# Value products of the DMA-transposed probability chunks: three 16-bit matmuls, or two 32-bit matmuls behind a GpSimd conversion

## The chip, the cores and the metric

The kernel runs on one core of one Trainium2 chip. The metric is the device time of one execution in microseconds (us); lower is better. Five engines work on the core at the same time, each through its own instructions in a fixed order: PE (TensorE, matrix products; PEld is its weight load), DVE (VectorE), ACT (ScalarE), POOL (GpSimd), and SP, which here only issues DMA transfers. An engine that waits for one instruction holds back everything behind it in its own order.

## The reference

One layer of an encoder is computed for two sequences, a sample of 512 tokens and a prompt of 1024 tokens, with model width 1024. What the change touches is the softmax attention of branch A: 8 query heads of width 64, in two groups of four that share one key and one value head each.

```python
def _gqa_attention(q, k, v):
    ...
    def block(qi):
        s = jnp.einsum('bqkgd,bskd->bkgqs', qi, k, preferred_element_type=jnp.float32) * scale
        p = jax.nn.softmax(s, axis=-1)
        return jnp.einsum('bkgqs,bskd->bqkgd', p.astype(v.dtype), v)
```

Everything is float32. The rest (projections, rotary embedding, a neighbourhood attention as branch B, gates, an MLP of width 4096, a final norm) is the same in both kernels.

## The kernel before

The kernel holds 32-bit accuracy with matmuls on split numbers: a value is cut into a high part in the 32-bit matmul format (`F32R`) and the remainder as a low part, and products of the parts are summed in PSUM. It runs the sample trunk, then the prompt trunk (`run`), then the MLP of both. Only the prompt trunk (`NB == 2`, so `ND = 4`) is touched.

In the prompt trunk each of the two head groups g has a phase phR, which projects q, k and v, rotates q and k, and writes the values into `vhl` (per chunk of 128 keys: 64 columns high part, 64 columns low part), and then a phase phA, the attention. phA walks over eight units of (head h, half of the queries qb); a unit is 512 queries against 1024 keys, that is eight key chunks. While the products of a unit are made, the scores of the next unit are computed (`s_tile`, four per unit, one per 128 queries):

- PE makes the scores (tile `ss`, four matmuls); DVE takes the negated row maximum (`nms`); ACT the exponential with its row sum (`ps`, `ls`); DVE the reciprocal (`rls`); POOL multiplies it by 2^14 (`rcs`).
- The last four key chunks go the DMA way: ACT writes `hls` high = p times `rcs` in float16, DVE the float16 remainder, and an SP-issued transposing DMA puts both into `PTs` (high and low plane of each chunk, keys on the partitions).
- The first four key chunks go the PE way: POOL normalises them (`pns`), and `turn` transposes them on PE (four 128x128 transposes into `pTs`), ACT copies the high part (`pths`) and DVE the remainder (`ptls`).

`pv` adds the value products of one chunk to the unit's accumulator `os`. For a PE-way chunk these are two matmuls with `vhl` (on `pths`, on `ptls`); for a DMA-way chunk three with 16-bit operands, straight from `PTs`: weights `vpls`, a bfloat16 three-part split of the value chunk that phR writes for the last four token tiles in `rotate` (ACT, DVE, two POOL operations per tile, and one memset per group). After the eighth chunk, `finish_o` adds the two halves and stores them.

Between these, `fill.pull` puts single k-steps (three matmuls into `gpss`) of the gate projection into PE's order, so that PE has work that depends on nothing in the unit: six k-steps per unit. The table `PLAN` gives, for each of eight slots of a unit, how many turns, how many scores of the next unit and how many products are emitted in program order. From program order a scheduler makes the final order of each engine; what is shown of orders below is that final one. Buffers: `pths` and `ptls` two each, `PTs` two, `hls` two, `pns` seven.

Of the kernel before, what the change touches and what calls it, by code (L numbers as in the profile page):

```python
# [10 lines left out]

F32 = mybir.dt.float32
F32R = mybir.dt.float32r
BF16 = mybir.dt.bfloat16
F16 = mybir.dt.float16
# [14 lines left out]
    (1, 1, (0, 0)),  # L30
    (1, 1, (0, 0)),
    (0, 0, (1, 0)),
    (1, 1, (1, 0)),
    (1, 0, (0, 1)),
    (0, 1, (1, 0)),
    (0, 0, (1, 1)),
    (0, 0, (0, 2)),
# [36 lines left out]
def encoder(ctx: ExitStack, tc: tile.TileContext, xs, outs, w):  # L74
# [367 lines left out]
    def run(tr, nxt, first):  # L442
# [79 lines left out]
        aside = ExitStack()  # L522
        if ND:
            vps = aside.enter_context(phase(f"vp{N}"))
        for g in range(2):
            with phase(f"phR{N}_{g}") as ph:
# [108 lines left out]
                if ND:  # L635
                    vpl = vps.tile([P, ND, 4, HD], BF16, tag="vp", name=f"vpl{N}_{g}", bufs=1)
# [46 lines left out]
                for tt in range(NT):  # L683
# [55 lines left out]
                    def rotate(tt, nm, z, zq, r, rt, pin):  # L739
                        if ND:  # L740
                            t6 = ph.tile([P, 6, HD], F32, tag="t", name=f"t{nm}", bufs=3)
                            t = t6[:, 0:5, :]
                        else:
                            t = ph.tile([P, 5, HD], F32, tag="t", name=f"t{nm}", bufs=2)
# [6 lines left out]
                        if tt >= NP:  # L751
                            if tt == NP:
                                tc.keep_in_program_order(nc.gpsimd.memset(vpl[:, :, 3, :], 0.0))
                            nc.scalar.activation(vpl[:, tt - NP, 0, :], z[:, 320:384], AF.Copy, scale=1.0 / PSC)
                            vr = t6[:, 5, :]
                            nc.vector.scalar_tensor_tensor(
                                vr, z[:, 320:384], 1.0 / PSC, vpl[:, tt - NP, 0, :], op0=ALU.mult, op1=ALU.subtract
                            )
                            nc.gpsimd.tensor_copy(vpl[:, tt - NP, 1, :], vr)
                            nc.gpsimd.tensor_tensor(vpl[:, tt - NP, 2, :], vr, vpl[:, tt - NP, 1, :], op=ALU.subtract)  # L760
                        else:
                            nc.scalar.activation(vhl[:, tt, 0:HD], z[:, 320:384], AF.Copy)
                            nc.vector.tensor_tensor(
                                vhl[:, tt, HD:P], z[:, 320:384], vhl[:, tt, 0:HD].bitcast(F32), op=ALU.subtract
                            )
# [12 lines left out]
                        if ND:  # L778
                            nc.vector.tensor_tensor(t, t, u, op=ALU.add)
                            nc.gpsimd.tensor_copy(t6[:, 5, :], t[:, 4, :])  # L780
                            rr_of[tt] = t6
                        else:
                            rr = ph.tile([P, 6, HD], F32, tag="rr", name=f"rr{nm}", bufs=3)
                            nc.vector.tensor_tensor(rr[:, 0:5, :], t, u, op=ALU.add)
                            nc.gpsimd.tensor_tensor(rr[:, 5, :], t[:, 4, :], u[:, 4, :], op=ALU.add)
                            rr_of[tt] = rr
# [27 lines left out]
            with phase(f"phA{N}_{g}") as ph:  # L814
# [3 lines left out]
                def s_tile(u, j):  # L818
# [33 lines left out]
                    pn = ph.tile([P, NP * P], F32, tag="PN", name=f"pn{nm}", bufs=7)  # L852
# [5 lines left out]
                def turn(u, kc):  # L858
# [5 lines left out]
                    nb = 2 if ND else 3  # L864
# [4 lines left out]
                    return hi, lo  # L869

# [21 lines left out]
                for j in range(4):  # L892
                    s_tile(units[0], j)
                    fill.pull(3 if ND else 2)
                queue = []
                for ui, u in enumerate(units):
                    h, qb = u
                    if first:
# [1137 lines left out]
```

## Time and profile before

| | |
|---|---|
| median of 3 runs (range) | 2125.79 us (2123.9 to 2126.83) |
| profiled execution: time, span | 2125.93 us, 2124.1 us |
| PE busy | 2100.1 us (99%) |
| DVE, ACT, POOL busy | 1473.8, 1122.3, 376.6 us (69%, 53%, 18%) |
| first score of the prompt's attention to its last value product, group 0, group 1 | about 450 to 569 us, 641 to 758 us |
| PE instructions / POOL instructions | 10775 / 590 |

The profiled execution is one run with the hardware profiler; its span runs from the first to the last instruction. "Busy" of PE is not PE at its peak, since matmuls overlap and the recorded end of a matmul lies behind the start of the next. In the rows of groups the columns are: line, engine, operation, output and inputs, shape, count, then busy time and mean ns of one, then the idle time ahead of them and what ended it. Buffer numbers are left out in the names.

### The profile page before, as it was taken

How to read it: one execution, taken by the hardware profiler on the slowest of the kernel's cores; microseconds unless marked ns; L12 is line 12 of the kernel's file. 1: busy time of each engine (PE TensorE's matmuls, PEld its weight loads, DVE VectorE, ACT ScalarE, POOL GpSimd, SP SyncE). 2: the span in 40 equal slices, each digit the busy share in tenths (PEclk: the TensorE clock that was granted, in tenths of full speed). 3: DMA queues.
4: the chain of work that ended last, by engine and by line, in shares of the span. 5: the costliest groups of instructions: out<-in, count | busy, mean ns of one | idle time of the engine just before them, and what ended most of it. 6: DMA issues, size and time to landing. Idle time of an engine off the chain costs nothing.

```text
span 2124.1 us, 31653 instructions
## 1 busy us (share of the span) xinstructions
PE 2100.1 (99%) x10775; PEld 1816.9 (86%) x10775; DVE 1473.8 (69%) x2810; ACT 1122.3 (53%) x2351; POOL 376.6 (18%) x590
## 2 busy tenths in 40 slices
PE   9999999999999999999999999999999999999998
PEld 8887778987796778888888999999999988888887
DVE  6675687777667755557772877778777777759563
ACT  5664664567547744555531666566555633334352
POOL 3232420432232223443201100002000000000000
PEclk9999999999999999999999999999999999999999
DMA  6435567644535443434473656578444799688561
GB/s 187 138 114 156 151 186 247 199 112 93 119 102 118 107 126 94 118 102 124 145 240 109 198 196 205 159 236 214 156 155 153 261 354 342 216 271 277 176 197 71
DMA packets 387178, 367.68 MB, mean 173 GB/s; under 512 B 98752, under 2 KB 322632, under 8 KB 387017
## 3 DMA queue, kind: packets, MB, share of 16 engines
q1 hardware_dynamic: 345079, 295.65, 46.4%
q10 hardware_dynamic: 36258, 52.98, 7.2%
q0 software_dynamic: 5680, 17.04, 2.9%
q8 instruction: 85, 1.39, 0.3%
q14 instruction: 76, 0.62, 0.1%
HBM read 264.85 MB, written 87.88 MB: 166 GB/s over the span
## 4 chain that ended last, share of the span: by engine, by line
PE 52%; DVE 1%; DMA 1%; ACT 1%; issue 0%; POOL 0%; ACTq 0%; POOLq 0%; DVEq 0%
PE dn L216 7%; PE dn L217 7%; PE dn L215 7%; PE uc L215 2%; PE ud L215 2%; PE ud L217 2%; PE uc L217 2%; PE ud L216 2%; PE uc L216 2%; PE ua L217 2%; PE ua L215 2%; PE ua L216 2%; PE ops L217 1%; PE ops L216 1%; PE ops L215 1%; PE ub L215 1%
## 5 line engine op out<-in xcount | busy, mean ns | idle before, releaser
L217 PE MATMUL dn<-wd,al 128*128 128x512 f32 (+1 forms) x624 | 242.3, 388 | 0.0
L216 PE MATMUL dn<-wd,ah 128*128 128x512 f32 (+1 forms) x624 | 242.3, 388 | 0.0
L215 PE MATMUL dn<-wd,ah 128*128 128x512 f32 (+1 forms) x624 | 242.3, 388 | 0.0
L1449 ACT ACTIVATE ah<-ar 128x512 fp32r<-128x512 f32 x168 | 104.5, 628 | 199.7 <-PE dn L216 184.8
L1450 DVE TENSOR_TENSOR al<-ar,ah 128x512 fp32r<-128x512 f32 x168 | 115.5, 694 | 72.8 <-ACT ah L1449 65.1
L215 PEld LDWEIGHTS dn<-wd,ah 128*128 128x128 f32 x624 | 117.2, 188 | 24.4
L216 PEld LDWEIGHTS dn<-wd,ah 128*128 128x128 f32 x624 | 117.2, 188 | 24.1
L217 PEld LDWEIGHTS dn<-wd,al 128*128 128x128 f32 x624 | 117.2, 188 | 24.0
L200 POOL TENSOR_TENSOR rs_f<-ms_f,mhalf 128x1 f32<-128x1 f32 x6 | 4.0, 666 | 590.7 <-DVE ms_f L196 590.7
L829 DVE TENSOR_REDUCE nms<-ss 128x1 f32<-128x1024 f32 (+1 forms) x96 | 99.7, 1040 | 12.0 <-PE ss L827 11.5
L832 ACT ACTIVATE ps<-ss,nms 128x1024 f32<-128x1024 f32 (+1 forms) x96 | 93.0, 969 | 26.5 <-DVE nms L829 12.9
L215 PE MATMUL gpss<-xs_0h,w_gs 128*128 128x512 f32 x256 | 103.5, 404 | 1.5 <-DVE ptls L868 1.3
L217 PE MATMUL gpss<-xs_0h,w_gs 128*128 128x512 f32 x256 | 100.8, 394 | 0.0
L216 PE MATMUL gpss<-xs_0l,w_gs 128*128 128x512 f32 x256 | 100.8, 394 | 0.0
L1449 ACT ACTIVATE A<-S 128x512 fp32r<-128x512 f32 x128 | 76.1, 624 | 32.1 <-DVE S L1512 26.6
L1450 DVE TENSOR_TENSOR A<-S,A 128x512 fp32r<-128x512 f32 x128 | 84.5, 686 | 4.8 <-ACT A L1449 4.8
L1568 ACT ACTIVATE c<-c 128x384 f32<-128x384 f32 x97 | 50.7, 524 | 68.8 <-DVE c L1567 68.5
L215 PE MATMUL uc<-B,A 128*128 128x384 f32 x256 | 85.6, 334 | 1.2 <-ACT s L1584 1.2
L215 PE MATMUL ud<-B,A 128*128 128x384 f32 x256 | 85.6, 334 | 0.0
L217 PE MATMUL ud<-B,A 128*128 128x384 f32 x256 | 85.5, 334 | 0.0
L216 PE MATMUL ud<-B,A 128*128 128x384 f32 x256 | 85.5, 334 | 0.0
L216 PE MATMUL uc<-B,A 128*128 128x384 f32 x256 | 85.5, 334 | 0.0
(376 smaller groups left out, 6396.5 us busy)
## 6 DMA issues: line engine op xcount, KB each, us to landing
ar<-ud SPq DMA_DIRECT2D x120, 512.0 KB
br<-in_w_mlp_down_dram SPq DMA_DIRECT2D x72, 512.0 KB
rawu<-in_w_mlp_up_dram SPq DMA_DIRECT2D x64, 512.0 KB
ud<-c ACTq DMA_DIRECT2D x128, 192.0 KB
raw_gs<-in_w_in_dram SPq DMA_DIRECT2D x32, 512.0 KB
zgs<-sgs ACTq DMA_DIRECT2D x48, 256.0 KB
ud<-cs SPq DMA_DIRECT2D x64, 192.0 KB
raw_os<-in_w_out_dram SPq DMA_DIRECT2D x16, 512.0 KB
```

The costliest lines, as they stand in the source:

```text
L200: nc.gpsimd.tensor_tensor(r[:, :n], m[:, :n], mhalf[:, :n], op=ALU.pow)
L215: nc.tensor.matmul(out, ah, bh, start=start, stop=False, **kw)
L216: nc.tensor.matmul(out, ah, bl, start=False, stop=False, **kw)
L217: nc.tensor.matmul(out, al, bh, start=False, stop=stop, **kw)
L829: nc.vector.tensor_reduce(nm_, s, axis=AX.X, op=ALU.max, negate=True)
L832: nc.scalar.activation(p, s, AF.Exp, bias=nm_, accum_out=l)
L1449: nc.scalar.activation(hi, src, AF.Copy)
L1450: nc.vector.tensor_tensor(lo, src, hi.bitcast(F32), op=ALU.subtract)
L1568: nc.scalar.activation(t, t, AF.Relu)
```

## The change

The DMA-way chunks now get the same two products with `vhl` as the others. For that POOL turns the two float16 planes of a chunk into 32-bit tiles (`widen`: two `tensor_scalar` of 128x512, tiles `pthd` and `ptld`, scaled by 2^-14), which share the buffers of `pths` and `ptls`; those now have three buffers each. `vpls` and its making in `rotate` are gone, so all eight token tiles write `vhl`; the sum of the rotation gets a tile `rr` of its own again. `pns` has six buffers instead of seven. `PLAN` has other columns (turns, scores, chunks to widen, products of turned chunks, products of widened chunks): the fourth turn and the third score change slots, and the last widened chunk's product stands at the start of the next unit.

```diff
-    (0, 0, (1, 0)),
+    (1, 0, (), 1, 0),
...
-                        if ND:
-                            t6 = ph.tile([P, 6, HD], F32, tag="t", name=f"t{nm}", bufs=3)
-                            t = t6[:, 0:5, :]
-                        else:
-                            t = ph.tile([P, 5, HD], F32, tag="t", name=f"t{nm}", bufs=2)
+                        t = ph.tile([P, 5, HD], F32, tag="t", name=f"t{nm}", bufs=2)
...
-                        if tt >= NP:
-                            if tt == NP:
-                                tc.keep_in_program_order(nc.gpsimd.memset(vpl[:, :, 3, :], 0.0))
-                            nc.scalar.activation(vpl[:, tt - NP, 0, :], z[:, 320:384], AF.Copy, scale=1.0 / PSC)
-                            vr = t6[:, 5, :]
-                            nc.vector.scalar_tensor_tensor(
-                                vr, z[:, 320:384], 1.0 / PSC, vpl[:, tt - NP, 0, :], op0=ALU.mult, op1=ALU.subtract
-                            )
-                            nc.gpsimd.tensor_copy(vpl[:, tt - NP, 1, :], vr)
-                            nc.gpsimd.tensor_tensor(vpl[:, tt - NP, 2, :], vr, vpl[:, tt - NP, 1, :], op=ALU.subtract)
-                        else:
...
+                        nc.scalar.activation(vhl[:, tt, 0:HD], z[:, 320:384], AF.Copy)
+                        nc.vector.tensor_tensor(
+                            vhl[:, tt, HD:P], z[:, 320:384], vhl[:, tt, 0:HD].bitcast(F32), op=ALU.subtract
+                        )
...
-                            nc.vector.tensor_tensor(t, t, u, op=ALU.add)
-                            nc.gpsimd.tensor_copy(t6[:, 5, :], t[:, 4, :])
...
+                        nc.vector.tensor_tensor(rr[:, 0:5, :], t, u, op=ALU.add)
+                        nc.gpsimd.tensor_tensor(rr[:, 5, :], t[:, 4, :], u[:, 4, :], op=ALU.add)
...
-                    pn = ph.tile([P, NP * P], F32, tag="PN", name=f"pn{nm}", bufs=7)
+                    pn = ph.tile([P, NP * P], F32, tag="PN", name=f"pn{nm}", bufs=6)
...
-                    nb = 2 if ND else 3
+                    nb = 3
...
+                def widen(u, i):
+                    res = []
+                    for e, tag in ((0, "pth"), (1, "ptl")):
+                        t = ph.tile([P, 512], F32R, tag=tag, name=f"{tag}d{N}_{g}_{u[0]}_{u[1]}_{i}", bufs=3)
+                        nc.gpsimd.tensor_scalar(t, PT[u][:, e * ND + i, :], 1.0 / PSC, None, op0=ALU.mult)
+                        res.append(t)
+                    return u, NP + i, res
...
-                    if hl is not None:
-                        nc.tensor.matmul(o, vhl[:, kc, :], hl[0], start=(n == 1), stop=False)
-                        nc.tensor.matmul(o, vhl[:, kc, :], hl[1], start=False, stop=(n == NT))
-                    else:
-                        v12 = vpl[:, kc - NP, 0:2, :].rearrange("p i d -> p (i d)")
-                        v30 = vpl[:, kc - NP, 2:4, :].rearrange("p i d -> p (i d)")
-                        nc.tensor.matmul(o, v12, PT[u][:, kc - NP, :], start=(n == 1), stop=False)
-                        nc.tensor.matmul(o, v12, PT[u][:, ND + kc - NP, :], start=False, stop=False)
-                        nc.tensor.matmul(o, v30, PT[u][:, kc - NP, :], start=False, stop=(n == NT))
+                    nc.tensor.matmul(o, vhl[:, kc, :], hl[0], start=(n == 1), stop=False)
+                    nc.tensor.matmul(o, vhl[:, kc, :], hl[1], start=False, stop=(n == NT))
...
+                        if ND and i == 0:
+                            while wide:
+                                pv(*wide.pop(0))
...
+                        for c in convs:
+                            wide.append(widen(u, c))
...
+                        for _ in range(pds):
+                            pv(*wide.pop(0))
```

How the order of two engines moves, at the end of one unit of the prompt (group 0, head 1, first query half; in the names of this place the last small number is the chunk or the query tile j, the long number is a tile counter). PE before, from the gate k-step ahead of the fourth turned chunk on (`pths_..._3`, `ptls_..._3`: that chunk; `ss_0_2_0_0`: the first score of the unit after the next; `PTs`, `vpls`: the DMA way; the first of the four DMA-way chunks stands earlier, and two more like the one that begins here follow):

```order
L215 MATMUL gpss_2304_2_0_5858<-xs_0h_4257,w_gs_2304_2_5452 128x512
L216 MATMUL gpss_2304_2_0_5858<-xs_0l_4259,w_gs_2304_2_5452 128x512
L217 MATMUL gpss_2304_2_0_5858<-xs_0h_4257,w_gs_2304_2_5452 128x512
L880 MATMUL os_0_1_0_5862<-pths_0_1_0_3_5901,vhls_0_4466 128x512 [waits Activation_49]
L826 MATMUL ss_0_2_0_0_5957<-kTs_0_4465,qTs_0_0_4463 128x512 [waits PE_49]
L827 MATMUL ss_0_2_0_0_5957<-kTs_0_4465,qTs_0_0_4463 128x512
L881 MATMUL os_0_1_0_5862<-ptls_0_1_0_3_5902,vhls_0_4466 128x512 [waits DVE_49]
L885 LDWEIGHTS vpls_0_4467
L885 MATMUL os_0_1_0_5862<-PTs_0_1_0_5643,vpls_0_4467 128x512
L886 LDWEIGHTS vpls_0_4467
L886 MATMUL os_0_1_0_5862<-PTs_0_1_0_5643,vpls_0_4467 128x512
L887 LDWEIGHTS vpls_0_4467
```

PE after, the same place (directly ahead of it stand the two products of the first widened chunk, `pthds_0_1_0_0` and `ptlds_0_1_0_0`):

```order
L215 MATMUL gpss_2304_2_0_5886<-xs_0h_4257,w_gs_2304_2_5447 128x512
L216 MATMUL gpss_2304_2_0_5886<-xs_0l_4259,w_gs_2304_2_5447 128x512
L217 MATMUL gpss_2304_2_0_5886<-xs_0h_4257,w_gs_2304_2_5447 128x512
L862 MATMUL os_0_1_0_5890<-pths_0_1_0_3_5904,vhls_0_4463 128x512 [waits Activation_49]
L863 MATMUL os_0_1_0_5890<-ptls_0_1_0_3_5905,vhls_0_4463 128x512 [waits DVE_49]
L862 MATMUL os_0_1_0_5890<-pthds_0_1_0_1_5928,vhls_0_4463 128x512 [waits Pool_49]
L863 MATMUL os_0_1_0_5890<-ptlds_0_1_0_1_5930,vhls_0_4463 128x512 [waits Pool_49]
L862 MATMUL os_0_1_0_5890<-pthds_0_1_0_2_5962,vhls_0_4463 128x512 [waits Pool_49]
L863 MATMUL os_0_1_0_5890<-ptlds_0_1_0_2_5964,vhls_0_4463 128x512 [waits Pool_49]
L862 MATMUL os_0_1_0_5890<-pthds_0_1_0_3_5976,vhls_0_4463 128x512 [waits Pool_49]
L801 MATMUL ss_0_2_0_0_5988<-kTs_0_4462,qTs_0_0_4460 128x512 [waits Activation_49]
L863 MATMUL os_0_1_0_5890<-ptlds_0_1_0_3_5978,vhls_0_4463 128x512 [waits Pool_49]
```

Behind the fourth turned chunk stood nine matmuls that wait for no engine of the unit; now there stand six, each of which waits for POOL.

POOL before, in the same unit (`rcs` and `pns` of the second, third and fourth query tile of the next unit, then of the unit after it):

```order
L842 TENSOR_SCALAR rcs_0_1_1_1_5841<-rls_0_1_1_1_5839 128x1 [waits DVE_49,Pool_49]
L853 TENSOR_SCALAR pns_0_1_1_1_5847<-ps_0_1_1_1_5836,rls_0_1_1_1_5839 128x512 [waits PE_49,Activation_49]
L842 TENSOR_SCALAR rcs_0_1_1_2_5886<-rls_0_1_1_2_5884 128x1 [waits DVE_49,Pool_49]
L853 TENSOR_SCALAR pns_0_1_1_2_5892<-ps_0_1_1_2_5881,rls_0_1_1_2_5884 128x512 [waits Activation_49]
L842 TENSOR_SCALAR rcs_0_1_1_3_5923<-rls_0_1_1_3_5921 128x1 [waits DVE_49]
L853 TENSOR_SCALAR pns_0_1_1_3_5929<-ps_0_1_1_3_5918,rls_0_1_1_3_5921 128x512 [waits Activation_49]
L842 TENSOR_SCALAR rcs_0_2_0_0_5969<-rls_0_2_0_0_5967 128x1 [waits DVE_49,Pool_49]
L853 TENSOR_SCALAR pns_0_2_0_0_5976<-ps_0_2_0_0_5964,rls_0_2_0_0_5967 128x512 [waits PE_49,Activation_49]
```

POOL after, the same place, from the second widened chunk on:

```order
L850 TENSOR_SCALAR pthds_0_1_0_1_5928<-PTs_0_1_0_5650 128x512 [waits PE_49,Pool_49]
L850 TENSOR_SCALAR ptlds_0_1_0_1_5930<-PTs_0_1_0_5650 128x512 [waits PE_49,Pool_49]
L850 TENSOR_SCALAR pthds_0_1_0_2_5962<-PTs_0_1_0_5650 128x512 [waits PE_49]
L850 TENSOR_SCALAR ptlds_0_1_0_2_5964<-PTs_0_1_0_5650 128x512 [waits PE_49]
L850 TENSOR_SCALAR pthds_0_1_0_3_5976<-PTs_0_1_0_5650 128x512 [waits DVE_49,PE_49]
L817 TENSOR_SCALAR rcs_0_1_1_2_5920<-rls_0_1_1_2_5918 128x1 [waits DVE_49]
L828 TENSOR_SCALAR pns_0_1_1_2_5926<-ps_0_1_1_2_5915,rls_0_1_1_2_5918 128x512 [waits Activation_49]
L850 TENSOR_SCALAR ptlds_0_1_0_3_5978<-PTs_0_1_0_5650 128x512 [waits PE_49]
L817 TENSOR_SCALAR rcs_0_1_1_3_5949<-rls_0_1_1_3_5947 128x1 [waits DVE_49]
L828 TENSOR_SCALAR pns_0_1_1_3_5955<-ps_0_1_1_3_5944,rls_0_1_1_3_5947 128x512 [waits Activation_49]
```

Five conversions stand ahead of `rcs` and `pns` of the third query tile (j = 2) and one more behind them; from `pthds_0_1_0_2` on, each conversion waits for PE to have read what was in its buffer (`pthds_0_1_0_2` takes the buffer of `pthds_0_1_0_0`, `pthds_0_1_0_3` that of the fourth turned chunk, `pths_0_1_0_3`).

## What the change will do: the prediction

> **What bounds the kernel now.** I read the page's busy times first, then the prompt's attention cut into stretches, then its groups of instructions, its waits, and last the timeline for the true pace of PE.
>
> ```profile
> PE 2100.1 (99%) x10775; PEld 1816.9 (86%) x10775; DVE 1473.8 (69%) x2810; ACT 1122.3 (53%) x2351; POOL 376.6 (18%) x590
> PEclk9999999999999999999999999999999999999999
> ```
>
> PE is busy nearly throughout, at full clock, and no other engine comes near; work taken off PE should shorten the time wherever nothing else takes the lead. The change touches only the prompt's attention. The next view gives, for six whole units of each head group (from the end of the first unit to the end of the seventh), length, then busy time and count of PE, PEld, DVE, ACT and POOL; its third row is a piece of the projection phase phR.
>
> ```profile
> 473.20:559.90 86.70, 85.24 (x422) 62.83 (x420) 68.27 (x107) 64.05 (x111) 21.64 (x50) 1.00 0.53 107
> 659.70:748.50 88.80, 86.31 (x422) 62.50 (x421) 69.30 (x108) 64.97 (x111) 21.26 (x50) 1.00 0.53 109
> 580.00:620.00 40.00, 40.00 (x280) 40.00 (x279) 23.43 (x78) 15.88 (x80) 17.24 (x31) 1.00 0.17 57
> ```
>
> A unit takes 86.7/6 = 14.45 us and 88.8/6 = 14.80 us, 14.62 on average. DVE is busy 68.27/6 = 11.4 us of it, POOL 3.6. To know what PE needs, its pace has to be read from starts in the timeline, since recorded matmuls overlap.
>
> ```profile
> 483.00 0.39 PE L215 MATMUL gpss<-xs_1h,w_gs 128*128 128x512 f32 x1
> ...
> 485.07 0.39 PE L881 MATMUL os<-ptls,vhls 128*128 128x512 f32 x1
> ...
> 485.30 0.39 PE L885 MATMUL os<-PTs,vpls 128*128 128x512 f16 x1
> ...
> 487.04 0.38 PE L887 MATMUL os<-PTs,vpls 128*128 128x512 f16 x1
> 480.51 0.60 PE L863 MATMUL pTs<-ident,pns 128*128 128x128 f32 x4
> ```
>
> The first two rows are nine 32-bit matmuls apart: 2.07/9 = 0.230 us each. The next two are eight 16-bit matmuls apart: 1.74/8 = 0.2175 us. A transpose takes about (0.60 - 0.27)/3 = 0.11 us. A unit has 16 score, 8 turned-chunk and 18 gate matmuls in 32 bits, 12 DMA-way matmuls and 16 transposes (70 instructions; 422/6 in the view): 42 x 0.230 + 12 x 0.2175 + 16 x 0.11 = 14.03 us. So PE sets the pace, with 0.6 us per unit in which it waits. What it waits for in group 0:
>
> ```profile
> PE os L881 <- DVE ptls L868: 1.2, 2, 1.0
> PE os L885 <- issue: 0.2, 1, 0.2
> ```
>
> **The change: what PE gains.** Four chunks per unit lose three 16-bit matmuls each and get two in 32 bits: 12 x 0.2175 - 8 x 0.230 = 0.77 us per unit, leaving 13.26 us of PE work. Over 16 units that is 12.3 us. It is real only where PE doesn't wait instead. The weights of the new products load more slowly:
>
> ```profile
> L880 PEld LDWEIGHTS os<-pths,vhls x96: 186/188/192, 64.6 to 755.1; 128*128 128x128 f32 x96
> L885 PEld LDWEIGHTS <-vpls x64: 95/97/98, 467.3 to 756.9; 128*128 128x128 bf16 x64
> ```
>
> 188 ns against 97 ns, both under the 230 ns of the matmul ahead, as it is with the turned chunks today; cost nothing.
>
> **What POOL gets.** 128 conversions of 128x512, 8 per unit, which the trace of before does not show. The nearest rows:
>
> ```profile
> L853 POOL TENSOR_SCALAR pns<-ps,rls 128x512 f32<-128x512 f32 x25 | 17.3, 692 | 0.0
> L842 POOL TENSOR_SCALAR rcs<-rls 128x1 f32<-128x1 f32 x25 | 5.1, 205 | 66.5 <-DVE rls L840 55.1 <-PE pTs L863 11.4
> L780 POOL COPY ts<-ts 128x64 f32<-128x64 f32 x16 | 4.1, 255 | 15.7 <-DVE ts L779 15.2 <-DVE ms_As L196 0.5
> L759 POOL CAST vpls<-ts 128x64 bf16<-128x64 f32 x8 | 2.1, 262 | 0.7 <-DVE ts L756 0.7
> L355 POOL TENSOR_TENSOR B<-ta,B 128x512 fp32r<-128x512 f32 x12 | 15.5, 1290 | 123.1 <-ACT B L352 120.5 <-DVE B L355 1.6 <-DMA xrs<-in_x_prompt_dram 1.0
> L1081 POOL TENSOR_TENSOR bms<-rects,msks 128x384 f32<-128x384 f32 x48 | 45.5, 949 | 77.7 <-DVE msbs L1097 71.5 <-DMA msks<-in_mask_dram 6.2
> L1081 POOL TENSOR_TENSOR bms<-rects,msks 128x256 f32<-128x256 f32 x24 | 18.0, 753 | 31.3 <-DVE msbs L1097 20.4 <-DMA rects<-biases 8.2 <-DVE rsbs L1104 2.5
> ```
>
> The same operation on the same tile in float32 takes 0.69 us, and at 64 columns a conversion to 16 bits costs what a copy does, so the width of the number seems to cost nothing. Writing the 32-bit matmul format is seen only in a two-input operation, 1.29 us; the two-input rows in float32 extrapolate to 753 + 2 x 196 = 1.15 us at 512 columns, so the format costs at most 1.29/1.15 = 12%. I take 0.69, the row of the same operation; the ends are 0.78 (with that 12%) and 0.45 (the 205 ns floor and half of the rest, should 16-bit input be read at double pace). Over the four conversions that close a unit (below) they move the sum by +5 and -13 us. POOL's load rises from 3.6 to 3.6 + 8 x 0.69 = 9.1 us per unit, which fits in 14. The Trainium skill's page GPSIMD Engine Reference, section 3.1, gives 769 ns as measured for a tight one-input loop over 512 elements; by that figure the four conversions below would cost an estimated 0.3 us more per unit, and the forecast would be about 4 us higher. The row of this trace, 692 ns, is what I use.
>
> **Where the order bites.** The orders shown above decide. Call t = 0 the start of the first widened product on PE (`pthds_0_1_0_0`). Its buffer goes to the third conversion pair, so `pthds_0_1_0_2` can start only when that matmul has ended, 0.39 us (the row above) plus about 0.1 for the hand-over: t = 0.5. Then POOL must do both planes of chunks 2 and 3: four conversions, 2.77 us, done at 3.3, and in this unit also `rcs` and `pns` of the third query tile, 0.205 + 0.692 = 0.9, done at 4.2. PE meanwhile has the second product of that chunk, three gate steps, two products of the turned chunk, four of widened chunks 1 and 2, one of chunk 3 and a score, 12 x 0.230 = 2.76 us, before it wants `ptlds_0_1_0_3`. It stalls for 4.2 + 0.1 - 2.76 = 1.5 us. I went through POOL's order for the other units: of the 14 that have a next unit, 12 have one such pair ahead of the last conversion and behind the second chunk's, 2 have none (3.3 + 0.1 - 11 x 0.230 = 0.8 us). Mean (12 x 1.5 + 2 x 0.8)/14 = 1.4 us of new waiting against 0.77 us saved.
>
> What of the 0.6 us of old waiting stays? While PE stalls, DVE and ACT go on, so part of the old waits for `ptls` goes. Against that, `rcs` of the third tile now stands behind five conversions. Its score is done 3 us before t = 0, and the chain to its reciprocal is
>
> ```profile
> L829 DVE TENSOR_REDUCE nms<-ss 128x1 f32<-128x1024 f32 x24 | 29.2, 1216 | 1.5 <-PE ss L827 1.2
> L832 ACT ACTIVATE ps<-ss,nms 128x1024 f32<-128x1024 f32 x25 | 27.8, 1110 | 7.5 <-DVE rls L840 3.1 <-DVE nms L829 2.5 <-DVE hls L846 1.8
> L832 ACT ACTIVATION_READ_ACCUMULATOR ps<-ss,nms 128x1 f32 x25 | 4.9, 194 | 0.0
> L840 DVE RECIPROCAL rls<-ls 128x1 f32<-128x1 f32 x25 | 4.0, 158 | 6.7 <-ACT ps L832 6.3
> ```
>
> 1.22 + 1.11 + 0.19 + 0.16 = 2.7 us, so it is ready near t = 0.2, but POOL comes to it at 0.5 + 3 x 0.69 = 2.6. Behind `rcs` wait ACT's `hls`, then DVE's, and in DVE's order behind that the next unit's first maximum; DVE's slack of 14.5 - 11.4 = 3.1 us per unit takes most of these 2.4 us, not all. I keep 0.35 of the 0.6. A full unit is then 13.26 + 1.4 + 0.35 = 15.0 us against 14.62; bounds 14.66 (nothing stays) and 15.26 (all stays). Fourteen units: +5.4 us, between +0.5 and +9. The last unit of each group has no next scores and no pair; it keeps part of its 0.77: -0.7 us for both.
>
> **Edits costed at nothing.** In phR the split of the value tiles loses POOL work and the sum of the rotation changes from copy to add; PE is 40.00 of 40.00 us busy there (row above), which hides it, up to about 0.3 us for each of 16 tiles, 4 us either way, without that cover. `pns` with six buffers makes the third next tile wait for the fourth turn, which stands on PE ahead of or among that tile's score; the tile isn't wanted for another 2.7 us. Third score and fourth turn change slots but not number. SP issues the same 64 transposes, and POOL frees `PTs` no later than PE did.
>
> Sum: 5.4 - 0.7 = +4.7 us on the profiled execution's 2125.93 (span 2124.1), which is 0.14 above the median of 2125.79: about 2131.
>
> **Rivals.** (1) *The chain on POOL is hidden*, as PE's share of the page suggests. It needs conversions of (2.76 - 0.6)/4 = 0.54 us where no pair intervenes, (2.16 - 0.9)/4 = 0.32 where one does, or products that lag so far that POOL is ahead. Then 12.3 us come off, 2114; with half of it 2120. For it: POOL is 18% busy. Against: the 692 ns.
> (2) *No change that can be told*: new waiting equals the saving, all old waiting is absorbed, 2126.
> (3) *POOL and DVE get in each other's way*. The rows for it, start and duration of each:
>
> ```profile
> 559.21 0.69 POOL L853 TENSOR_SCALAR pns<-ps,rls 128x512 f32<-128x512 f32 x1
> 559.34 1.10 DVE L846 SCALAR_TENSOR_TENSOR hls<-ps,rcs,hls 128x512 f16<-128x512 f32 x1 [0.45 <-ACT hls L845]
> 462.75 0.75 DVE L846 SCALAR_TENSOR_TENSOR hls<-ps,rcs,hls 128x512 f16<-128x512 f32 x1 [0.22 <-ACT hls L845]
> 462.85 1.21 POOL L853 TENSOR_SCALAR pns<-ps,rls 128x512 f32<-128x512 f32 x1
> ```
>
> Where `hls` on DVE (two inputs from SBUF) and a POOL operation overlap, the one that starts second is stretched: DVE from 0.75 to 1.10, POOL from 0.69 to 1.21. Today POOL is busy a quarter of a unit; after, three fifths (9.1 of 15). If two POOL operations of each closing chain are hit, 2 x 0.52 x 14 = 14.6 us come on top: 2146. One hit per unit gives 2138. It decides if `hls` falls into the closing chain. The Trainium skill's page Advanced Engine Details and Errata, section GPSIMD Details, states it as a shared read and write interface, in conflict with DVE instructions that have two SBUF inputs; by that rule the trace agrees for `hls`, and such hits are to be expected.
>
> **How the numbers follow.** About 0.2% (4.3 us) is what a measurement of this kernel can tell from no change. Main case 0.35, rival 3 0.15, both slower: 0.50. Rival 2: 0.28. Rival 1: 0.22. The likeliest case is the main one, 2131, by itself 2126 to 2135. For eight in ten I reach down to 2117 (conversions at their lower end, and half of rival 1's chance) and up to 2147 (rival 3 with two hits, or one hit and conversions at their upper end).
>
> **What would show it.** Right: PE waits of 0.8 to 1.5 us for POOL's `ptlds` or `pthds` near the end of a unit, units of about 15.0 us, POOL near 465 us in all, the conversion at 0.69. Wrong: units of 13.5 us with no waits for POOL (rival 1), conversions far from 0.69, or `hls` and conversions stretched past 1 us throughout (rival 3).

## The result, and the profile after

The changed kernel takes 2264.33 us (median of 4 runs, 2262.59 to 2265.32) against 2125.86 for the kernel before beside it: a ratio of 1.0652, with a 95% interval of 1.0633 to 1.067. That is 138.5 us slower, where 2131 was predicted and the range ended at 2147. Its profiled execution took 2264.96 us, with a span of 2263.2.

The page of the changed kernel, its busy times and its row of PE's granted clock in 40 slices:

```profile
PE 2157.9 (95%) x10711; PEld 1852.5 (82%) x10711; DVE 1486.0 (66%) x2810; ACT 1123.0 (50%) x2351; POOL 568.4 (25%) x700
PEclk9999999988789787999999999999999999999999
```

PE executes 64 matmuls fewer and yet is busy for 57.8 us longer, and the clock row, all nines before, falls to 7 and 8 in the slices of the prompt's attention. Both have one place. The view of stretches, for the same six whole units of each head group as in the prediction (from the last product of the first unit to that of the seventh; columns as there: length, busy time and count of PE, PEld, DVE, ACT, POOL, then the granted clock):

```profile
481.57:620.00 138.43, 106.63 (x397) 76.09 (x396) 74.26 (x106) 63.79 (x109) 92.96 (x97) 0.80 0.33 69
738.54:877.73 139.19, 106.89 (x397) 76.26 (x397) 73.68 (x106) 63.92 (x108) 93.94 (x97) 0.79 0.32 67
```

A unit takes (138.43 + 139.19)/12 = 23.1 us, where it took 14.62. PE's idle time, length minus busy time, is (31.80 + 32.30)/12 = 5.3 us per unit against 0.33 before, by the prediction's rows (1.46 + 2.49 us in twelve units). Its busy time is 17.8 us against 14.3, for 0.77 us less work. So a unit has lost 5.0 us to idle time and 3.5 us in which PE is recorded as busy. The last unit of each group, which has no scores beside it, takes 19.7 and 19.3 us against 9.2 and 9.3. What PE waits for, and what one conversion costs (the view of one line: minimum, median, maximum in ns):

```profile
PE os L863 <- POOL ptlds L850: 44.0, 50, 2.0
PE os L862 <- POOL pthds L850: 35.7, 35, 2.3
```

```profile
L850 POOL TENSOR_SCALAR pthds<-PTs x64: 1487/1488/2017, 466.4 to 893.2; 128x512 fp32r<-128x512 f16 x64
L850 POOL TENSOR_SCALAR ptlds<-PTs x64: 1487/1488/1761, 468.0 to 894.7; 128x512 fp32r<-128x512 f16 x64
```

The wait is the one that the prediction named, at 80 us in all, and the conversion is not what it took: 1.49 us, not 0.69, with nearly no spread. POOL in the timeline at the end of a unit, and PE in the same place (start, duration):

```profile
519.61 1.49 POOL L850 TENSOR_SCALAR pthds<-PTs 128x512 fp32r<-128x512 f16 x1
521.18 1.49 POOL L850 TENSOR_SCALAR ptlds<-PTs 128x512 fp32r<-128x512 f16 x1
522.75 1.49 POOL L850 TENSOR_SCALAR pthds<-PTs 128x512 fp32r<-128x512 f16 x1
```

```profile
521.15 0.79 PE L862 MATMUL os<-pthds,vhls 128*128 128x512 f32 x1 [0.21 <-POOL pthds L850]
522.72 0.79 PE L863 MATMUL os<-ptlds,vhls 128*128 128x512 f32 x1 [0.77 <-POOL ptlds L850]
524.29 0.79 PE L862 MATMUL os<-pthds,vhls 128*128 128x512 f32 x1 [0.77 <-POOL pthds L850]
```

Each product on PE starts at the end of the conversion that feeds it, one per 1.57 us. After such waits PE does not go on at its usual 0.230 us per matmul. From the timeline one unit earlier:

```profile
503.38 0.79 PE L863 MATMUL os<-ptlds,vhls 128*128 128x512 f32 x1 [0.35 <-POOL ptlds L850]
503.97 0.63 PE L802 MATMUL ss<-kTs,qTs 128*128 128x512 f32 x1
504.40 0.63 PE L801 MATMUL ss<-kTs,qTs 128*128 128x512 f32 x1
504.82 0.63 PE L802 MATMUL ss<-kTs,qTs 128*128 128x512 f32 x1
505.25 0.63 PE L215 MATMUL gpss<-xs_1h,w_gs 128*128 128x512 f32 x1
```

Four matmuls that wait for nothing start 0.43 us apart. That is the second loss. It is not the whole of the 3.5 us: a product that stands alone between two waits counts as busy with its full recorded length, 0.79 us, and how the 3.5 us divide was not measured.

The granted clock is not a little lower throughout; it changes between full and half. The view of stretches again, cut where it changes:

```profile
495.70:499.11 3.41, 1.01 (x2) 0.37 (x2) 0.16 (x1) 0.37 (x2) 3.25 (x3) 1.00 0.40 77
499.11:505.94 6.83, 4.58 (x9) 2.87 (x10) 2.21 (x3) 1.93 (x3) 4.83 (x7) 0.50 0.20 38
505.94:519.59 13.65, 11.25 (x55) 8.52 (x55) 8.63 (x13) 7.74 (x13) 7.69 (x8) 1.00 0.35 80
519.59:529.83 10.24, 7.20 (x14) 3.97 (x15) 4.28 (x7) 4.23 (x8) 7.66 (x8) 0.50 0.20 37
```

Each of the 16 units has one stretch at half clock, 6.83 or 10.24 us long, twice or three times 3.41 us, and it begins at the end of the unit, where PE waits for POOL. Cut into pieces of 3.41 us on the same grid, the trace has PE busy for 20 to 43% of the piece ahead of each of the 16 drops; no piece with PE busy for 57% or more has a drop behind it.

### The profile page after: what moved, and what is told of

It is laid out like the page before. It is cut to its first block, busy times and chain, and to the rows that moved or that the text cites. A ratio compares the mean times of both kernels' runs of the same rounds, so it can differ in the third digit from the quotient of the medians.

```text
span 2263.2 us, 31598 instructions
## 1 busy us (share of the span) xinstructions
PE 2157.9 (95%) x10711; PEld 1852.5 (82%) x10711; DVE 1486.0 (66%) x2810; ACT 1123.0 (50%) x2351; POOL 568.4 (25%) x700
## 5 line engine op out<-in xcount | busy, mean ns | idle before, releaser
L821 DVE SCALAR_TENSOR_TENSOR hls<-ps,rcs,hls 128x512 f16<-128x512 f32 x64 | 58.2, 917 | 79.9 <-ACT hls L820 79.7
L850 POOL TENSOR_SCALAR pthds<-PTs 128x512 fp32r<-128x512 f16 x64 | 97.6, 1525 | 39.9 <-PE os L862 20.8
L820 ACT ACTIVATE hls<-ps,rcs 128x512 f16<-128x512 f32 x64 | 45.9, 720 | 110.3 <-POOL rcs L817 107.4
L850 POOL TENSOR_SCALAR ptlds<-PTs 128x512 fp32r<-128x512 f16 x64 | 95.9, 1498 | 5.1
L1060 POOL TENSOR_TENSOR bms<-rects,msks 128x384 f32<-128x384 f32 (+1 forms) x72 | 63.5, 885 | 108.6 <-DVE msbs L1076 91.6
L215 PE MATMUL uc<-B,A 128*128 128x384 f32 x256 | 85.6, 334 | 1.2 <-ACT s L1563 1.2
```

The costliest lines, as they stand in the source:

```text
L215: nc.tensor.matmul(out, ah, bh, start=start, stop=False, **kw)
L820: nc.scalar.activation(hl[:, 0, :], pd, AF.Copy, scale=rlc)
L821: nc.vector.scalar_tensor_tensor(hl[:, 1, :], pd, rlc, hl[:, 0, :], op0=ALU.mult, op1=ALU.subtract)
L850: nc.gpsimd.tensor_scalar(t, PT[u][:, e * ND + i, :], 1.0 / PSC, None, op0=ALU.mult)
L1060: nc.gpsimd.tensor_tensor(bm.rearrange("p (r c) -> p r c", c=32), rects[h][:, ir : ir + kr_n, jr : jr + 32], msk[:, hf * 3 + ct, :].rearra ...
```

## The experiments

**What makes the conversion dear.** The prediction took 0.69 us from `pns`, the same operation name on POOL on the same tile size. They differ in the input (16 bits against 32), in the output (32-bit matmul format against float32), and in the form: `pns` multiplies by a 128x1 operand and then by 1.0, the conversion only once, by an immediate. Twelve forms were put at the start of the prompt's encoder of the kernel before, among them (written short):

```diff
+ nc.gpsimd.tensor_scalar(out("qa", F32R), s16, 1.0 / PSC, None, op0=ALU.mult)
+ nc.gpsimd.tensor_scalar(out("qd", F32), s32, 1.0 / PSC, None, op0=ALU.mult)
+ nc.gpsimd.tensor_scalar(out("qe", F32), s32, one, 1.0, op0=ALU.mult, op1=ALU.mult)
+ nc.gpsimd.tensor_scalar(out("qf", F32), s16, one, 1.0, op0=ALU.mult, op1=ALU.mult)
+ nc.gpsimd.tensor_scalar(out("qh", F16), s16, 1.0 / PSC, None, op0=ALU.mult)
+ nc.gpsimd.tensor_copy(out("qi", F32), s16)
+ nc.vector.tensor_scalar(out("qk", F32R), s16, 1.0 / PSC, None, op0=ALU.mult)
+ nc.scalar.activation(out("ql", F32R), s16, AF.Copy, scale=1.0 / PSC)
```

> The kernel before, with twelve forms of a 128x512 conversion issued four times each at the start of the prompt's encoder; their outputs are not used. The changed kernel's conversion (16-bit float in, 32-bit matmul format out, one immediate operand) took 1.49 us where the prediction had 0.69, the row of pns (float32 in and out, a pointer operand and two operations). Theory I (the input): the 16-bit float source costs the extra time; then every form that reads 16-bit floats takes about 1.5 us, whatever it writes, and every form that reads float32 about 0.7. Theory O (the output): the 32-bit matmul format costs it; then the forms that write it take 1.5 and those that write float32 or 16 bits 0.7, whatever they read. Theory F (the form): one immediate and one operation cost it; then float32 to float32 in that form takes 1.5 too. DVE and ACT are measured on the same conversion beside it: I expect 0.6 us or less on each.

The groups of that run (four instructions each; busy us, mean ns; the first `qa` ran beside DVE work and lifts its mean):

```profile
L98 POOL TENSOR_SCALAR qa<-s 128x512 fp32r<-128x512 f16 x4 | 6.1, 1536 | 0.3
L101 POOL TENSOR_SCALAR qd<-s 128x512 f32<-128x512 f32 x4 | 5.9, 1487 | 0.3
L105 POOL TENSOR_SCALAR qh<-s 128x512 f16<-128x512 f16 x4 | 5.9, 1487 | 0.3
L102 POOL TENSOR_SCALAR qe<-s,one 128x512 f32<-128x512 f32 x4 | 2.8, 692 | 0.4
L103 POOL TENSOR_SCALAR qf<-s,one 128x512 f32<-128x512 f16 x4 | 2.8, 691 | 0.0
L106 POOL CAST qi<-s 128x512 f32<-128x512 f16 x4 | 2.4, 609 | 0.3
L108 DVE TENSOR_SCALAR qk<-s 128x512 fp32r<-128x512 f16 x4 | 2.6, 639 | 0.4 <-POOL s L87 0.3
L109 ACT ACTIVATE ql<-s 128x512 fp32r<-128x512 f16 x4 | 2.5, 629 | 0.1
```

The formats cost nothing: 16 bits to the matmul format, float32 to float32, 16 bits to 16 bits all take 1.49 us in the one-operation form. With a 128x1 operand and two operations, both inputs take 0.69; the plain cast 0.61. DVE, beside POOL's work, does the same conversion in 0.64 and ACT in 0.63. So it was the form, which left two traits: the immediate, or the single operation. Ten further forms were measured in the same place, among them (written short):

```diff
+ ra: tensor_scalar(out F32R, s16, one, 1.0, op0=mult, op1=mult)
+ rb: tensor_scalar(out F32R, s16, one, None, op0=mult)
+ rc: tensor_scalar(out F32R, s16, 1.0 / PSC, 1.0, op0=mult, op1=mult)
+ rd: tensor_scalar(out F32R, s16, one, one, op0=mult, op1=mult)
+ re: tensor_copy(out F32R, s16)
+ rf, rg: as the changed kernel's conversion, 256 and 64 columns;  rh: as ra, 256 columns
```

> The kernel before, with ten further forms of the conversion, four times each, outputs unused. Which trait of the immediate form doubles its time? Theory immediate: two immediates and two operations stay at 1.49 us, a 128x1 operand with one operation takes 0.69. Theory one operation: two immediates with two operations take 0.69, a 128x1 operand with one operation 1.49. At 256 columns a price that is all per column gives 0.75 us for the immediate form, at 64 columns 0.19; with a floor of 0.2 us 0.85 and 0.36. The pointer form into the 32-bit matmul format: 0.69.

The second repeat in the timeline of POOL, in the order ra to rh:

```profile
9.85 0.69 POOL L98 TENSOR_SCALAR ra<-s,one 128x512 fp32r<-128x512 f16 x1
10.51 1.56 POOL L99 TENSOR_SCALAR rb<-s,one 128x512 fp32r<-128x512 f16 x1
12.16 0.62 POOL L100 TENSOR_SCALAR rc<-s 128x512 fp32r<-128x512 f16 x1
12.88 0.76 POOL L101 TENSOR_SCALAR rd<-s,one 128x512 fp32r<-128x512 f16 x1
13.59 0.61 POOL L102 CAST re<-s 128x512 fp32r<-128x512 f16 x1
14.29 0.85 POOL L103 TENSOR_SCALAR rf<-s 128x256 fp32r<-128x256 f16 x1
15.22 0.37 POOL L104 TENSOR_SCALAR rg<-s 128x64 fp32r<-128x64 f16 x1
15.68 0.48 POOL L105 TENSOR_SCALAR rh<-s,one 128x256 fp32r<-128x256 f16 x1
```

It is the single operation. One operation takes 1.56 us with a 128x1 operand; two operations take 0.62 with two immediates, 0.69 and 0.76 with operands. By the widths, one operation costs (1.49 - 0.37)/448 = 2.5 ns per column, two operations (0.69 - 0.48)/256 = 0.8. The Trainium skill's page GPSIMD Engine Reference, section 3.1, has 769 ns, as its best case, for a tight loop over 512 elements. The form with two 128x1 operands, 0.76 us, agrees with it; the other two-operation forms and the cast, 0.61 to 0.69 us, lie up to a fifth under it, and the one-operation form takes twice as much.

**The input format alone, in place.** The same instruction with the same waits, but reading 512 float32 numbers from the same bytes (a scale that keeps them small; what it writes is not the softmax's weights):

```diff
- nc.gpsimd.tensor_scalar(t, PT[u][:, e * ND + i, :], 1.0 / PSC, None, op0=ALU.mult)
+ pp = (e * ND + i) // 2 * 2
+ nc.gpsimd.tensor_scalar(t.rearrange(...), PT[u][:, pp : pp + 2, :].bitcast(F32), 2.0**-107, None, op0=ALU.mult)
```

> The changed kernel, with each conversion reading 512 float32 numbers from the same buffer's bytes instead of 512 16-bit ones (scaled so that they stay small); it waits for the same transposes and writes the same tiles, but what it writes is not the weights of the softmax, so the output is not the reference's. Theory I (the 16-bit source makes the conversion dear): conversions near 0.70 us, POOL near 465 us in all, units near 15.0 us, and the time the prediction's sum, about 2131 us; if the waits of PE also lower its clock, up to 2150. Theory O or F (the output format or the form makes it dear): conversions stay at 1.49 us and the time at 2264.

Measured: 2251.58 us, a ratio of 1.0594 (1.0579 to 1.061). The groups:

```profile
L851 POOL TENSOR_SCALAR pthds<-PTs 128x512 fp32r<-128x512 f32 x64 | 97.4, 1522 | 35.2 <-PE os L865 27.9 <-DMA PTs<-hls 5.9 <-POOL pns L828 0.9
L851 POOL TENSOR_SCALAR ptlds<-PTs 128x512 fp32r<-128x512 f32 x64 | 96.6, 1510 | 0.0
```

The price stays, and nearly all of the loss with it, so the input is cleared in place too. That it is still 12.8 us faster than the changed kernel no theory here explains; the granted clock in the stretches of six units is 0.82 there, against 0.80 and 0.79.

**The price put right.** The changed kernel with the conversion in the form of `pns`:

```diff
+ isc = ph.tile([P, 1], F32, tag="isc", name=f"isc{N}_{g}", bufs=1)
+ nc.gpsimd.memset(isc, 1.0 / PSC)
- nc.gpsimd.tensor_scalar(t, PT[u][:, e * ND + i, :], 1.0 / PSC, None, op0=ALU.mult)
+ nc.gpsimd.tensor_scalar(t, PT[u][:, e * ND + i, :], isc, 1.0, op0=ALU.mult, op1=ALU.mult)
```

> The changed kernel with one edit: the conversion multiplies by a 128x1 operand that holds 2^-14 and then by 1.0, as pns does, instead of by one immediate. In the measurement of single forms that took 0.69 us where the immediate took 1.49. Theory price (the conversion's 1.49 us is the whole error, and the rest of the prediction's sum holds): POOL near 465 us, PE waits of 0.8 to 1.5 us at the ends of units, units near 15.0 us, 2131 us, within 2126 to 2135. Theory clock too (waits of that size lower PE's granted clock as well): 14 units lose another 1 to 2 us, 2145 to 2160. Theory chain hidden (PE's older waits absorb it): 2114.

Measured: 2149.62 us (2147.76 to 2150.8), a ratio of 1.0113 (1.0099 to 1.0127). The line of the conversion, PE's waits for it, and the stretches of six units:

```profile
L852 POOL TENSOR_SCALAR pthds<-PTs,iscs x64: 684/692/1664, 468.3 to 781.1; 128x512 fp32r<-128x512 f16 x64
L852 POOL TENSOR_SCALAR ptlds<-PTs,iscs x64: 684/692/1641, 468.9 to 781.8; 128x512 fp32r<-128x512 f16 x64
```

```profile
PE os L864 <- POOL pthds L852: 10.0, 17, 2.3
PE os L865 <- POOL ptlds L852: 9.7, 22, 1.1
```

```profile
476.26:571.89 95.63, 86.41 (x396) 65.87 (x396) 72.58 (x106) 63.62 (x108) 58.75 (x97) 0.98 0.48 97
674.83:771.68 96.85, 88.50 (x398) 67.93 (x397) 72.67 (x106) 63.52 (x108) 59.85 (x96) 0.95 0.46 95
```

With the conversion at its 0.692 us, 114.7 of the 138.5 us are gone. What is left is the kernel that the prediction described, and it is 23.8 us slower than before, not 5; that lies in the range of the second theory, the clock, though the row of the clock covers only a part of it (below). A unit takes (95.63 + 96.85)/12 = 16.0 us, 15.0 predicted. PE's idle time in it is (9.22 + 8.35)/12 = 1.46 us, where the prediction had 1.4 + 0.35. Its busy time is 14.6 us for 13.26 us of work, and the granted clock 0.98 and 0.95: this was not in the sum. Instead of one stretch at half clock in each unit there are four in all, of 3.41 us each. POOL is at 474.6 us on this kernel's page, about 465 predicted.

With two immediates, the cheapest form (one argument changed, `None` to `1.0` with a second `mult`):

> The changed kernel with a second operation in the conversion (times 2^-14, then times 1.0, both immediates), which took 0.62 us singly against 1.49 for one operation alone and 0.69 with the 128x1 operand. Theory price: the time follows the conversion's price; against the kernel with 0.69 us (2149.6) four conversions of each of 14 closing chains are 0.07 us shorter: 3.9 us, about 2146. Theory that the remainder above the kernel before (24 us) is not the closing chain: no change, 2149.

Measured: 2148.96 us, 1.012 (1.0105 to 1.0136), units of (97.93 + 95.16)/12 = 16.1 us, the conversion at a median of 0.62. Another 0.07 us off each conversion buys nothing that can be told, so the remaining loss is no simple multiple of the price.

**Does the slow clock cost anything, or does it only fill time in which PE would wait?** Products of zeros, added into the same accumulator ahead of each widened product, three each in the changed kernel:

```diff
+ z = ph.tile([P, HD], F32R, ...); nc.gpsimd.memset(z.bitcast(F32), 0.0)
  for e in range(2):
+     if ND and kc >= NP:
+         for _ in range(3):
+             nc.tensor.matmul(o[0:HD, :], z, kT[:, e, 0:512], start=False, stop=False)
      nc.tensor.matmul(o, vhl[:, kc, :], hl[e], ...)
```

> The changed kernel, with three further products ahead of each widened product on PE: a stationary tile of zeros (64 columns) against the keys, added into the same accumulator, so the sum is unchanged. That is 384 matmuls, 88 us of PE work at 0.230 us each. They only fill time in which PE would wait. Theory clock (each wait costs twice, because PE runs at half pace for some us after it): the granted clock in the attention rises from 0.75 to 0.88 there towards 1, and the time falls in spite of the added work, to about 2235 us. Theory wait alone (POOL's 1.49 us sets the end, PE's low clock costs nothing that it would not wait anyway): no fall, 2264 us where the zeros fit in the waits, and up to 2352 where they do not.

Measured: 2248.48 us, 1.0578 (1.0563 to 1.0594): 384 matmuls more, and 15.9 us less than the changed kernel. The same stretches:

```profile
482.32:613.84 131.52, 119.13 (x541) 85.07 (x541) 78.65 (x106) 63.70 (x108) 92.42 (x96) 0.99 0.36 72
729.93:860.82 130.89, 118.56 (x542) 85.00 (x541) 79.21 (x106) 64.25 (x108) 92.38 (x96) 0.99 0.37 73
```

The clock goes from 0.80 to 0.99, with three stretches of 3.41 us at half clock left, and a unit from 23.1 to (131.52 + 130.89)/12 = 21.9 us, with conversions still at 1.49 and 24 x 0.230 = 5.5 us of work added per unit. PE now idles 2.1 us instead of 5.3. So work that fills the waits restored the clock, and the time fell, though by less than I expected (2235). How much of the fall is the clock's is not shown, since the run differs in one thing more: the scheduler made another order. In the changed kernel's full units up to eight conversions stand in POOL's order with no `rcs` or `pns` among them, here at most four.

In a small dose (one product of zeros ahead of each product of chunks 2 and 3, on top of the two-immediate form):

> The run with two immediates (2149.0), with one product of zeros ahead of each of the four widened products of chunks 2 and 3: 64 matmuls, 14.7 us of PE work that adds nothing to the sum. By the rows of the run with the 128x1 operand, a full unit of 16.0 us is 13.26 us of work at full pace, 1.3 us of waits for POOL, and about 1.0 us in which matmuls start more than 0.23 us apart behind a wait. Theory clock: the zeros take up to 0.9 of the 1.3 us of waits and most of the slow starts go: units of 15.1 to 15.5, 2136 to 2142 us. Theory wait alone: nothing falls, 2149 us or up to 15 more.

Measured: 2146.7 us, 1.0105 (1.0088 to 1.0121).

```profile
475.36:569.88 94.52, 89.67 (x422) 67.73 (x421) 73.08 (x106) 64.14 (x109) 56.92 (x98) 1.00 0.48 101
674.21:768.86 94.65, 90.01 (x421) 67.61 (x421) 73.23 (x106) 64.41 (x109) 57.00 (x97) 1.00 0.50 99
```

The clock is 1.00 and a unit (94.52 + 94.65)/12 = 15.8 us, against 16.1, with 0.92 us more of work in it. The direction is the clock theory's, and the 14.7 us of added work cost nothing, but the gain of 2.3 us is within the two intervals, and short of the 2136 to 2142 that I expected. PE's busy time less the zeros is still 14.05 us, 0.8 above its work, so part of the remainder is not the clock. Here too the order on POOL is another one than in the run without zeros, so even this gain is not the clock's alone.

**Must PE wait for the widened tiles, or is POOL's queue enough?** The kernel before, with the conversions on POOL in the changed slots into a tile that nobody reads (and six `pns` buffers, as after):

```diff
+ if ND and i in (3, 4, 6, 7):
+     widen(u, (3, 4, 6, 7).index(i))      # two tensor_scalar into a tile "wx", one operation each
- pn = ph.tile(..., bufs=7)
+ pn = ph.tile(..., bufs=6)
```

> The kernel before, with the 128 conversions added on POOL in the changed kernel's slots, into a tile that nobody reads (and with six buffers for pns instead of seven, as in the changed kernel). PE does not wait for them; only what stands behind them on POOL (rcs, pns) comes later. If the time of the changed kernel is lost because PE waits for the widened tiles: no more than 2126 to 2160 us here, with PE's waits for POOL near zero. If POOL's load itself does it (rcs and pns late, or its sharing a port with DVE): above 2200 us, with PE waiting for turned chunks and scores.

Measured: 2242.61 us, 1.0556 (1.0538 to 1.0573). I had expected 2126 to 2160 by the theory that I held. PE's waits:

```profile
PE pTs L863 <- POOL pns L853: 40.6, 21, 5.3
PE os L885 <- ACT pths L867: 19.1, 6, 5.1
PE ss L826 <- ACT ps L832: 13.1, 5, 5.5
```

Nothing on PE depends on the conversions here, and 117.6 us are lost all the same: `rcs` and `pns` stand behind runs of up to seven conversions in POOL's order, of which four take 6.3 us, and the turned chunks, the high parts and the scores come late with them. What having six `pns` buffers instead of seven adds is not known, since no run has that edit alone. The changed kernel has this path too:

```profile
ACT hls L820 <- POOL rcs L817: 107.4, 38, 6.9
```

The same with the two-operation form (a 128x1 operand):

> The kernel before with the 128 conversions added on POOL in the changed kernel's slots, read by nobody, now in the form of 0.69 us. With the form of 1.49 us this took 2242.6 us, with PE waiting for pns behind the conversions on POOL. If that was the queue (up to four conversions ahead of rcs and pns, 6 us): now up to 2.8 us ahead, mostly inside the slack of pns, 2126 to 2135 us. If it was POOL's use of the port that it shares with DVE: the same bytes move, so a good part stays, above 2160.

Measured: 2165.25 us, 1.0187 (1.0173 to 1.0201); I had expected 2126 to 2135 from the queue alone, and above 2160, as it came out, from POOL's conflict with DVE. PE's waits for `pns` fall to a quarter, but don't go:

```profile
PE pTs L865 <- POOL pns L855: 10.1, 9, 2.3
PE ss L828 <- ACT ps L834: 5.7, 4, 2.5
```

Of the 39.9 us that stay, this run does not tell how much is the queue, how much the six buffers, and how much POOL and DVE in each other's way: the unread conversions average 0.75 us there, and DVE's `hls` 0.89 against 0.78 before.

**A version that beats both?** The high planes on ACT, the low planes on POOL with the 128x1 operand:

```diff
+ if e == 0:
+     nc.scalar.activation(t, PT[u][:, i, :], AF.Copy, scale=1.0 / PSC)
+ else:
+     nc.gpsimd.tensor_scalar(t, PT[u][:, ND + i, :], isc, 1.0, op0=ALU.mult, op1=ALU.mult)
```

> The changed kernel with the high planes converted by ACT (0.63 us each when measured singly) and the low planes by POOL with the 128x1 operand (0.69). The four conversions that close a unit become two on each engine: 0.5 + 2 x 0.69 + 0.9 on POOL, 2.8 us, against PE's 2.76. If the closing chain on POOL alone holds PE up: PE's waits nearly go, and the time is 2114 to 2120. If ACT, whose load rises from 10.7 to 13.2 us per unit, becomes the late one (its exponentials and high parts stand in the same order): PE waits for ACT's pths and 2126 to 2150.

Measured: 2125.18 us, 0.9996 (0.9987 to 1.0006), as fast as before. PE's waits for widened tiles are nearly gone, as the first theory had it, and yet the time is not 2114 to 2120.

```profile
475.09:563.15 88.06, 84.17 (x399) 64.71 (x400) 68.49 (x107) 76.31 (x135) 39.32 (x73) 1.00 0.54 106
661.18:751.45 90.27, 84.52 (x397) 64.62 (x398) 69.52 (x108) 77.05 (x135) 40.22 (x73) 1.00 0.52 105
```

The last unit of each group, which has no scores beside it, falls from 9.21 and 9.27 us to 6.91 and 7.36, but that is not a saving: in this order half of its 16 transposes and more than half of its gate matmuls stand ahead of the end of the unit before it, so by the prediction's paces an estimated 5.0 and 5.7 us of PE work are left in it, where it had 8.7. A full unit does not fall: (88.06 + 90.27)/12 = 14.86 us against 14.62. The clock is 1.00, but PE idles 0.80 us per unit against 0.33, in many short waits (for `pns`, for DVE's `ptls`, for ACT), and its busy time is 14.06 against 14.29, 0.23 less where the work is 0.77 less. With two immediates on POOL:

> As the run with the high planes on ACT and the low planes on POOL (2125.2, PE's waits for widened tiles nearly gone, and no gain), but with the two-immediate form on POOL. If POOL's part still held it up: 2122 or less. If ACT's order (exponentials behind conversions that wait for the DMA transposes) eats the saving: 2125, the same.

Measured: 2125.84 us, 0.9999 (0.999 to 1.0008): the same, so POOL's price was not what held it. With only the high planes of chunks 2 and 3 on ACT, the rest on POOL:

> POOL converts both planes of chunks 0 and 1 and the low planes of chunks 2 and 3 (two immediates), ACT only the high planes of chunks 2 and 3, which close a unit. ACT no longer waits for the DMA transposes, and its load rises by 1.3 us per unit instead of 2.5. If ACT's order ate the saving: 2114 to 2121. If POOL's four early conversions ahead of rcs and pns cost as much: 2124 to 2132.

Measured: 2134.72 us, 1.0044 (1.0032 to 1.0057). Full units are the same, 14.90 us; the last ones take 11.41 and 10.19 us, 7.3 us more in the two together than in the first split (6.91 and 7.36). About 4.4 us of that is work: here all or most of the transposes stand in them again (16 and 13) and more gate matmuls. The rest was not taken apart. None of the three beats the kernel before.

## Why the prediction was wrong

**The step that failed** is the price under "What POOL gets": "The same operation on the same tile in float32 takes 0.69 us ... I take 0.69, the row of the same operation". It was not the same operation. The trace calls both TENSOR_SCALAR, but `pns` has two operations and the conversion has one, which the code printed ahead shows and no row of the profile does. One operation takes 1.49 us. My ends, 0.45 and 0.78, were drawn from formats, the trait that costs nothing, so the range could not hold it: 83% of the loss, 114.7 of 138.5 us, goes with the form (0.69 us in its place), and as much, 115.4 us, with the one argument that makes it two operations with immediates.

**The second step that failed** is the sum per unit, "13.26 + 1.4 + 0.35 = 15.0 us". It charged a wait of PE at its own length. With the right price PE idles 1.46 us, where the two terms of waiting made 1.75: that term held. But its busy time is 14.6 us for 13.26 of work, 1.3 above, where it was 0.26 above before (14.29 for 14.03). With the granted clock at 0.965 on average, about 0.5 of these 1.3 us is the clock, an estimate from the row (0.035 x 14.6); the rest is time in which PE is recorded as busy, and it is not taken apart further. Two smaller points of this sum: the 0.1 us for a hand-over stood in no row, and is about 0.05 us in the changed kernel (a conversion ends at 521.10, its product starts at 521.15); and by POOL's order one of the twelve units with a pair of `rcs` and `pns` ahead of the last conversion has two, which adds under 1 us to the whole.

**The last unit of a group** was put at -0.7 us for both. With the right price they lose 4.4 (11.52 + 11.35 against 9.21 + 9.27 us): in PE's order there is no score and little else beside the closing chain, which is the likely reason but was not tested. With the start of the two groups (2.9 and 0.9 us) and the full units (17.0), that is the whole 25 us by which the attention ends later.

**What held, and what no run shows.** The place of the new wait held: the end of a unit, for `ptlds` and `pthds` on POOL, with the pair of `rcs` and `pns` within the chain. The saving of 0.77 us of PE work a unit is a count of matmuls, and no run shows it as time: in the first split kernel, where PE's waits for widened tiles are nearly gone, PE's busy time is 0.23 us lower in a full unit and the unit 0.24 us longer. That `rcs` stands behind conversions I saw, and kept 0.35 us of a unit for it; at 1.49 us the unread conversions were worth 117.6 us, with POOL's queue, its conflict with DVE and the six `pns` buffers together. This can't be added to PE's waits, since both come from the same conversions. The edits in phR, costed at nothing, show in the start of the second group, 0.9 us later in relation to the end of the first, waits of its first unit included.

**The rivals.** The hidden chain needed 0.54 us or less, and 0.62 is the cheapest that was run in place of it; even so it stayed at 2149. The contention between POOL and DVE is there: `hls` takes 0.78 us on average before and 0.92 after, and with the right form the conversions average 0.80 against a median of 0.69, with single ones up to 1.66. It is not what the 114.7 us hung on, since these came off with the form alone. But rival 3 put the kernel with conversions of 0.69 us at 2138 to 2146, it measured 2149.6, and no run separates the contention's part of the 23.8 us that remain; it stays open.

## What to carry to other kernels

Price a new instruction by a row of the same form, operand kinds and number of operations included, not by a row of the same name; where none exists, bound it from both sides by every trait that differs, and measure that form singly before scheduling around it. Charge a pause of TensorE at more than its length: work behind it can run at half pace. A kernel with the pauses filled by useless products was 15.9 us faster here, though its order had changed too. When an engine that is 18% busy gets new work, look at what stands in its order behind that work: here the same work cost 117.6 us with nobody waiting for its result.

## What the runs showed of the hardware

POOL's elementwise operation with one scalar and one operation takes 1.49 to 1.56 us on 128x512, and with a second, useless multiplication 0.62 to 0.76 (a plain cast 0.61), in all the formats tried. A 128x1 operand in place of an immediate adds 0.07 us each time.

PE's clock falls after pauses that are short: in the changed kernel no single wait for POOL was longer than 2.3 us, and matmuls behind them started 0.43 us apart instead of 0.23. What goes with the drop is the share of 3.41 us in which PE is busy, 20 to 43% ahead of the 16 drops, and the clock stays at half for 6.83 or 10.24 us. With the right price the four drops had 42 to 56% ahead of them, so these runs give no sharp limit. The Trainium skill's page TensorE: Matmul & The Clock Gate, Part 1, gives half rate as the state after an idle window of about 3.4 us. The half pace and the 3.41 us agree with the trace; but the window ahead of a drop was not idle throughout, and no single pause was as long as that. The share of idle time over a longer stretch does not tell the clock: it was 0.80 with PE idle 23% of the six units, but 0.95 to 0.98 with 9%, and 0.99, also with 9%, once zeros filled the waits for POOL.
